# Seven block products instead of eight in two feed-forward expansions, with the inner features kept in DRAM

## Chip, cores and metric

The kernel runs on one core of a Trainium2 chip. The metric is the device time of one execution in microseconds, and the median over runs counts. Everything is float32 in and out, for 1024 tokens of 1024 features.

## What is computed

The program is a chain of three residual blocks. Only the feed-forward ends of the second and third block are touched (D_MODEL = 1024, D_FF = 2816, D_FF_3 = 4096):

```python
# second block
h = h + merged @ w_out[l]
hn = rmsnorm_2(h, norm_ffn[l])
g, up = jnp.split(hn @ w_ffn_in[l], 2, axis=-1)
h = h + (jax.nn.silu(g) * up) @ w_ffn_out[l]
return rmsnorm_2(h, norm_final)

# third block
m = rmsnorm_3(h, norm_mlp_g[l]) @ w_mlp_up[l].astype(h.dtype)
h = h + jnp.square(jax.nn.relu(m)) @ w_mlp_down[l].astype(h.dtype)
out = rmsnorm_3(h, norm_final_g)
```

The product with `w_ffn_in` or `w_mlp_up` is called the expansion here, the one with `w_ffn_out` or `w_mlp_down` the contraction.

## The kernel before

Activations lie feature-major: a tile has 128 features on the partitions and tokens along the row, in two halves `h` of 512 tokens, and eight such tiles `k` make the 1024 features. Every float32 operand of TensorE is split in two parts, a rounded copy (ScalarE, L76 for weights, L151 for activations) and the remainder (VectorE, L77 and L152). `mm3` (L142 to L144) then makes three matmuls of 512 columns per pair of tiles: high by high, high by low, low by high. So a product of one 128-feature output tile with 512 tokens takes 24 matmuls when the inner length is 1024, and 12 when it is 512.

`Weights` streams the weights in the order in which they are used: `load_to` issues a 512 KB load on SyncE's queue into one of two `wraw` buffers, `split_to` makes the two parts in one of four `wsplit` buffers, `get` hands out the next unit and splits one ahead. `gemm_fm` computes expansion units (24 matmuls into a PSUM tile `mm`, of which there are two, then the eviction `evict`); the first `lag` units go over half 0 of the tokens before half 1, since half 1 of the normalised input comes later. `gemm_out` computes the contraction, eight output tiles by two halves, each 3 x nk matmuls, and adds into the residual tiles `u` (L1117, L1480). `seam` is the `gemm_out` that ends a residual part: it takes half 0 completely before half 1, squares and sums each new `u` tile (ScalarE, with the running sum `acc` on GpSimd, L183), and starts `norm_gen` for each half. That makes the row of factors on TensorE (`tp`), copies it to SBUF (`rbc`), multiplies each `u` tile by it (`nt`, VectorE, L301) and splits the result into `xs[k, h]`.

In the second block each hidden tile needs a gate unit and an up unit (L383, L384, L1163), and the contraction follows in groups of 2, 4, 4, 4, 4, 4 hidden tiles (`FF_GROUPS`); one hidden tile of the next group is computed ahead of each group's contraction and the others behind it. In the third block it is eight groups of four, with a squared ReLU (L1497, L1498). Hidden tiles are split as they are made and stay in SBUF until their group is contracted. Residual tiles, `xs` and split hidden tiles take their space from the pools `pg` (28 pages of 4 KB a partition) and `px`.

A scheduler that follows dependencies and priorities writes each engine's instruction order once, ahead of time; evictions have a higher priority (`PRIO_E`). On the chip each engine, and each engine's DMA queue, works strictly in that order.

## Time and profile before

| what | value |
|---|---|
| runs shown, median | 3450.02 us (3443.96, 3450.02, 3455.81) |
| profiled execution | 3442.71 us, with a span of 3441.0 us on the core |
| mean granted TensorE clock | 0.993 |
| TensorE busy (matmul) | 3343.3 us, 16447 records |
| TensorE weight loads | 2730.7 us |
| VectorE / ScalarE / GpSimd busy | 1732.3 / 1054.0 / 249.8 us |
| DMA | 245.06 MB, mean 71 GB/s |

Busy time of TensorE counts overlapping matmuls, so the distance between their starts says more than the busy time of one. The second block's feed-forward part lies at about 1587 to 2297 us of the span, the third block's at about 2700 to 3420 us.

### The profile page before, as it was taken

What the parts mean: (1) busy time and instruction counts of PE and PEld (TensorE: products, weight loads), DVE (VectorE), ACT (ScalarE), POOL (GpSimd) and SP (SyncE); (2) the same over time, 40 slices, a digit from 0 to 9 for tenths busy, and PEclk for the clock granted to TensorE, in tenths of its full rate; (3) what the DMA queues carried; (4) which work ended last, traced back from release to release, by engine and by line L of the source; (5) the groups of instructions that cost most, each with busy time, mean ns of one, the idle gap of its engine ahead of it and who ended that gap; (6) DMA issues with size and microseconds to landing.
All of it is one profiled execution on the core that took longest, in us unless ns stands there. A gap on an engine that the chain in (4) does not pass through costs nothing.

```text
span 3441.0 us, 41019 instructions
## 1 busy us (share of the span) xinstructions
PE 3343.3 (97%) x16447; PEld 2730.7 (79%) x16447; DVE 1732.3 (50%) x3299; ACT 1054.0 (31%) x1853; POOL 249.8 (7%) x239
## 2 busy tenths in 40 slices
PE   6999999999999999999999999999999999999998
PEld 6788877677778888887788888878878788888887
DVE  7465556665655561546332333355569833333334
ACT  5222344433444432213111111144543421121122
POOL 0000000003000000112000000040211200000002
PEclk9999999999999999999999999999999999999999
DMA  5223211322111253421111111121112011111111
GB/s 185 63 99 128 89 51 41 110 68 95 60 40 45 83 166 137 145 80 51 56 49 49 49 49 50 49 95 53 46 50 86 34 53 49 44 48 49 50 49 56
DMA packets 98384, 245.06 MB, mean 71 GB/s; under 512 B 12945, under 2 KB 31505, under 8 KB 98193
## 3 DMA queue, kind: packets, MB, share of 16 engines
q1 hardware_dynamic: 84816, 199.92, 17.0%
q0 software_dynamic: 11360, 39.80, 3.4%
q8 instruction: 129, 2.11, 0.3%
q10 hardware_dynamic: 2016, 2.72, 0.2%
q14 instruction: 63, 0.51, 0.0%
HBM read 196.20 MB, written 46.20 MB: 70 GB/s over the span
## 4 chain that ended last, share of the span: by engine, by line
PE 82%; DVE 8%; issue 7%; ACT 2%; DMA 1%; POOL 0%; POOLq 0%; DVEq 0%; SPq 0%; ACTq 0%
PE mm L142 24%; PE mm L143 24%; PE mm L144 23%; DVE sp L152 1%; PE mm L1614 1%; DVE nt L301 1%; DVE wsplit L77 1%; PE sc L1213 1%; PE tp L1232 1%; PE tp L142 1%; PE tp L143 1%; PE tp L191 1%; PE tp L144 1%; PE sc L934 1%; DVE wsplit L1596 0%
## 5 line engine op out<-in xcount | busy, mean ns | idle before, releaser
L142 PE MATMUL mm<-sp,wsplit 128*128 128x512 f32 x3424 | 1362.0, 398 | 15.7 <-DVE u L1117 4.1
L143 PE MATMUL mm<-sp,wsplit 128*128 128x512 f32 x3424 | 1345.8, 393 | 12.1 <-DVE sp L152 9.6
L144 PE MATMUL mm<-sp,wsplit 128*128 128x512 f32 x3424 | 1343.4, 392 | 0.0
L142 PEld LDWEIGHTS mm<-sp,wsplit 128*128 128x128 f32 x3424 | 645.7, 189 | 157.0 <-issue 6.7
L143 PEld LDWEIGHTS mm<-sp,wsplit 128*128 128x128 f32 x3424 | 646.6, 189 | 144.3 <-DVE sp L152 14.5
L144 PEld LDWEIGHTS mm<-sp,wsplit 128*128 128x128 f32 x3424 | 645.9, 189 | 133.5 <-issue 0.4
L76 ACT CAST wsplit<-wraw 128x1024 fp32r<-128x1024 f32 x264 | 276.8, 1048 | 678.0 <-PE mm L144 632.6
L77 DVE TENSOR_TENSOR wsplit<-wraw,wsplit 128x1024 fp32r<-128x1024 f32 x264 | 330.6, 1253 | 176.2 <-ACT wsplit L76 174.1
L183 POOL TENSOR_TENSOR acc<-acc,sqt 128x512 f32<-128x512 f32 (+1 forms) x105 | 141.1, 1356 | 1523.1 <-ACT sqt L182 1436.5
L143 PE MATMUL mm<-hid,wsplit 128*128 128x512 f32 (+1 forms) x544 | 207.1, 381 | 0.0
L142 PE MATMUL mm<-hid,wsplit 128*128 128x512 f32 (+1 forms) x544 | 206.8, 380 | 0.0
L144 PE MATMUL mm<-hid,wsplit 128*128 128x512 f32 (+1 forms) x544 | 206.3, 379 | 0.0
L1480 DVE TENSOR_TENSOR u<-u,mm 128x512 f32<-128x512 f32 x144 | 98.8, 686 | 184.9 <-PE mm L144 184.6
L1117 DVE SCALAR_TENSOR_TENSOR u<-mm,u 128x512 f32<-128x512 f32 x128 | 88.0, 690 | 170.0 <-PE mm L144 170.0
L1498 DVE TENSOR_TENSOR hd<-hd 128x512 f32<-128x512 f32 x64 | 44.3, 693 | 189.4 <-ACT hd L1497 189.4
L142 PEld LDWEIGHTS mm<-hid,wsplit 128*128 128x128 f32 x544 | 102.2, 188 | 21.2
L143 PEld LDWEIGHTS mm<-hid,wsplit 128*128 128x128 f32 x544 | 102.5, 188 | 20.6
L144 PEld LDWEIGHTS mm<-hid,wsplit 128*128 128x128 f32 x544 | 102.2, 188 | 20.3
L384 DVE SCALAR_TENSOR_TENSOR silu<-silu,mm 128x512 f32<-128x512 f32 x44 | 30.3, 688 | 163.5 <-ACT silu L383 163.5
L1497 ACT ACTIVATE hd<-mm 128x512 f32<-128x512 f32 x64 | 38.3, 598 | 219.6 <-PE mm L144 219.6
L1163 DVE TENSOR_TENSOR silu<-silu,mm 128x512 f32<-128x512 f32 x44 | 30.3, 688 | 127.3 <-PE mm L144 127.3
L383 ACT ACTIVATE silu<-mm 128x512 f32<-128x512 f32 x44 | 26.3, 598 | 183.2 <-PE mm L144 183.2
(515 smaller groups left out, 3732.4 us busy)
## 6 DMA issues: line engine op xcount, KB each, us to landing
wraw<-W SPq DMA_DIRECT2D x264, 512.0 KB, 3.2
x_d<-u SPq DMA_DIRECT2D x32, 256.0 KB, 2.0
t_d<-gl SPq DMA_DIRECT2D x32, 256.0 KB, 2.0
u<-x_d POOLq DMA_DIRECT2D x16, 512.0 KB, 6.0
gl<-t_d POOLq DMA_DIRECT2D x32, 256.0 KB, 3.1
x<-xT SPq DMA_DIRECT2D x16, 256.0 KB, 5.4
u<-xT POOLq DMA_DIRECT2D x8, 512.0 KB, 5.6
bias<-bias POOLq DMA_DIRECT2D x4, 640.0 KB, 4.3
```

The lines of the kernel that those rows point to most:

```text
L76: K.nc.scalar.copy(s[:, 0, :], r)
L77: K.nc.vector.tensor_sub(s[:, 1, :], r, s[:, 0, :].bitcast(F32))
L142: t.matmul(ps, wh, xh, start=first, stop=False)
L143: t.matmul(ps, wh, xl, start=False, stop=False)
L144: t.matmul(ps, wl, xh, start=False, stop=last)
L152: nc.vector.tensor_sub(lo, src, hi.bitcast(F32))
L183: eng.tensor_add(acc, acc, t[:, :acc.shape[-1]])
L191: self.nc.tensor.matmul(ps[:, off + t:off + t + 1], acc[:, t * 128:(t + 1) * 128], self.ones[:, 0:1], start=True, stop=True)
L1117: nc.vector.scalar_tensor_tensor(uu(m, h), ps, 0.5, uu(m, h), op0=OP.mult, op1=OP.add)
L1480: nc.vector.tensor_add(uu(m, h), uu(m, h), ps)
L1497: nc.scalar.activation(t, ps, AF.Relu)
L1498: nc.vector.tensor_mul(t, t, t)
```

## The change

The expansion's weights are seen as blocks of two rows (two output tiles) by two columns (inner features 0 to 511 and 512 to 1023), and the tokens as blocks of two rows (the same feature halves) by two columns (token halves). Each such step of four output blocks needed eight block products of 12 matmuls; in Strassen's scheme in Winograd's form it takes seven, P1 to P7, with sums of blocks as operands. The sums of weights are made on GpSimd for each step (`ssum`, four instructions), those of tokens once per feed-forward part, on VectorE and GpSimd, in place in the `u` tiles (`block_tokens`, T1 to T4). The four outputs C11, C12, C21, C22 share products, so P1, P6, P7 and P4 accumulate in one PSUM tile that is read out in between, and P5 and P3 in half of another; VectorE adds the parts.

The first four units of each part are still computed plainly, with `lag=4`; then come 20 steps in the second block (one hidden tile each, gate and up) and 14 in the third (two hidden tiles each). No contraction stands between them: finished hidden halves go to DRAM (`store`, SyncE's queue), as do the `u` tiles during the seam, since their space is taken for the sums. When all steps are done, `down_loads` brings `u` and the hidden tiles back on GpSimd's queue, splits the latter, and the contractions follow one after the other, each group's loads issued up to one group ahead. The weights' order in DRAM follows. Weight loads for the steps use a third kind of buffer besides `wr` (`paged`).

```diff
+    def take(self, n):
+        j = self.given
+        self.load_to(j + 2 * n)
+        self.given = self.split = j + n
+        return [self.raw.pop(j + i) for i in range(n)]
...
+    def block_tokens(self, u, xs, gens, B, pages):
+        nc = self.nc
+        for k in range(4):
+            B["B11", k], B["B21", k], B["B22", k] = xs[k, 0], xs[k + 4, 0], xs[k + 4, 1]
...
+        for k in range(4):
+            nc.vector.tensor_sub(u(k, 0), u(k, 1), u(k, 0))
+            nc.gpsimd.tensor_sub(u(k, 1), u(k + 4, 1), u(k, 1))
+            part("T1", k, u(k, 0))
...
+        for k in range(4):
+            nc.vector.tensor_sub(u(k + 4, 1), u(k + 4, 1), u(k, 0))
+            nc.gpsimd.tensor_sub(u(k + 4, 0), u(k + 4, 0), u(k + 4, 1))
+            part("T2", k, u(k + 4, 1))
...
+        for n, o, h in (("T3", 0, 1), ("T4", 4, 0)):
...
+    def block_gemm(self, n, B, page, out):
+        nc = self.nc
+        seq = [("P1", 0), ("P5", 0)]
+        for i in range(n):
+            if i + 1 < n:
+                seq += [("P2", i), ("P6", i), ("P3", i), ("P1", i + 1), ("P7", i), ("P5", i + 1), ("P4", i)]
+            else:
+                seq += [("P6", i), ("P3", i), ("P2", i), ("P7", i), ("P4", i)]
+        moving = dict(P1="B11", P2="B21", P3="B22", P4="T4", P5="T1", P6="T2", P7="T3")
...
+            if p == "P5":
+                nc.gpsimd.tensor_add(s, a21, a22)
+                nc.gpsimd.tensor_sub(s3, a11, a21)
+            elif p == "P6":
+                nc.gpsimd.tensor_sub(s, s, a11)
+            elif p == "P3":
+                nc.gpsimd.tensor_sub(s, a12, s)
...
+            self.split(w, o, 512, dict(P1=a11, P2=a12, P4=a22, P7=s3).get(p, s))
...
+            for q in range(len(ready), min(j + 6, len(seq))):
+                ready[q] = operand(q)
...
+            for k in range(4):
...
+                for y, (c, e) in enumerate(((0, 0), (0, 1), (1, 0))):
+                    nc.tensor.matmul(d, wk[:, c, :], xk[:, e, :], start=new and k == y == 0, stop=k == 3 and y == 2,
+                                     skip_group_check=not new)
+            with self.tc.high_priority(offset=PRIO_E):
+                if p == "P1":
+                    nc.scalar.copy(x[:, 0, :], a)
+                elif p == "P5":
+                    nc.scalar.copy(x[:, 1, :], f)
+                elif p == "P2":
+                    nc.vector.tensor_add(x[:, 0, :], x[:, 0, :], b)
...
+                elif p == "P7":
+                    nc.vector.tensor_add(x[:, 1, :], x[:, 1, :], a)
...
+    def down_loads(self, u, u_d, pages, hid, hid_d, groups):
+        nc, m = self.nc, 0
+        for g, n in enumerate(groups):
+            while g > self.down + 1:
+                yield
+            if g < 2:
+                for k in range(4 * g, 4 * g + 4):
+                    u[k] = pages[0](name="ur")
+                    nc.gpsimd.dma_start(u[k], u_d[k])
...
+            for k in range(n):
+                raw.append(pages[1](name="hraw"))
+                nc.gpsimd.dma_start(raw[k], hid_d[m + k])
...
+        self.block_up(uu, xs, gens, B, dict.fromkeys(("T1", "T2", "T3", "T4"), self.split_page), ev_up)
+        for _ in self.block_gemm(20, B, page, out):
+            self.tick()
...
+        dl = self.spawn(self.down_loads(u2, u2_d, (self.xpage, self.page), hid, hid_d, FF_GROUPS))
...
-                up(m0 + n, 1)
                 for _ in self.gemm_out(src3, n, ev_add):
                     self.tick()
-                if FF_GROUPS[gi + 1] > 1:
-                    up(m0 + n + 1, FF_GROUPS[gi + 1] - 1)
...
+        for _ in self.gemm_fm(4, lambda k, h: xs[k, h], ev, lag=4, wait=xs, ahead=False):
+            self.tick()
```

Three places in the instruction order matter. Lines of `mm3`, `split` and `norm_gen` have moved down in the changed file (L142 to L149, L152 to L159, L301 to L436); L358 is the matmul of `block_gemm`.

TensorE, in the middle of the second block's expansion. Before, the end of one unit and the start of the next (`sp_13341`, `sp_13346`: tiles of `xs`):

```order
L142 MATMUL mm_14187<-sp_13619,wsplit_14091 128x512
L143 MATMUL mm_14187<-sp_13619,wsplit_14091 128x512
L144 MATMUL mm_14187<-sp_13619,wsplit_14091 128x512
L142 MATMUL mm_14219<-sp_13341,wsplit_14154 128x512 [waits DVE_49]
L143 MATMUL mm_14219<-sp_13341,wsplit_14154 128x512
L144 MATMUL mm_14219<-sp_13341,wsplit_14154 128x512
```

Now, P5 of one step (`sc_14240`, tokens T1) and P4 of the step before it (`mm_14068`, tokens T4):

```order
L358 MATMUL sc_14240<-sp_13646,wsplit_14123 128x512 x3
L358 MATMUL sc_14240<-sp_13651,wsplit_14123 128x512 x3
L358 MATMUL sc_14240<-sp_13669,wsplit_14123 128x512 x3
L358 MATMUL sc_14240<-sp_13674,wsplit_14123 128x512 x3
L358 MATMUL mm_14068<-sp_13779,wsplit_14160 128x512 [waits DVE_49]
L358 MATMUL mm_14068<-sp_13779,wsplit_14160 128x512 x2
L358 MATMUL mm_14068<-sp_13782,wsplit_14160 128x512 x3
L358 MATMUL mm_14068<-sp_13798,wsplit_14160 128x512 x3
L358 MATMUL mm_14068<-sp_13801,wsplit_14160 128x512 x3
```

A unit of 24 matmuls with one wait has become products of 12; the wait of P4 is for VectorE's read of `mm_14068` after P7, which stands right before this P5.

VectorE, behind the second block's normalisation of half 1. Before, the last normalised tiles are split, and ordinary evictions and weight splits follow:

```order
L301 SCALAR_TENSOR_TENSOR nt_13612<-u2_12359,vec_87,rbc_13539 128x512
L301 SCALAR_TENSOR_TENSOR nt_13617<-u2_12378,vec_87,rbc_13539 128x512 [waits DVE_49]
L152 TENSOR_TENSOR sp_13614<-nt_13612,sp_13614 128x512 [waits Activation_49]
L152 TENSOR_TENSOR sp_13619<-nt_13617,sp_13619 128x512 [waits Activation_49]
L384 SCALAR_TENSOR_TENSOR silu_13482<-silu_13482,mm_13599 128x512 [waits Activation_49]
L77 TENSOR_TENSOR wsplit_13697<-wraw_13411,wsplit_13697 128x1024 [waits DMAHW5_49,PE_49,Activation_49]
```

Now, further down (`wsplit_13823` holds the weights of P1 and P5 of the first step, `wsplit_13830` those of P2 and P6, `sp_13722` belongs to T2, `sp_13739` to `sp_13761` are T3):

```order
L159 TENSOR_TENSOR wsplit_13823<-wraw_13421,wsplit_13823 128x512 [waits DMAHW7_49,PE_49]
L1307 TENSOR_TENSOR silu_13689<-silu_13689,mm_13702 128x512 [waits PE_49]
L159 TENSOR_TENSOR sp_13722<-u2_12378,sp_13722 128x512 [waits Activation_49]
L159 TENSOR_TENSOR sp_13739<-u2_12233,sp_13739 128x512 [waits Activation_49]
L159 TENSOR_TENSOR sp_13742<-u2_12252,sp_13742 128x512 [waits Activation_49]
L159 TENSOR_TENSOR sp_13758<-u2_12275,sp_13758 128x512 [waits Activation_49]
L159 TENSOR_TENSOR sp_13761<-u2_12294,sp_13761 128x512 [waits Activation_49]
L159 TENSOR_TENSOR wsplit_13823<-ssum_13822,wsplit_13823 128x512
L159 TENSOR_TENSOR wsplit_13830<-wraw_13421,wsplit_13830 128x512 [waits Activation_49]
```

The operand of P5, TensorE's second product, has come to stand behind all the sums and splits of T1 to T3.

GpSimd, at the end of the second block's expansion. Before, its queue holds nothing between the running sums of the two seams but one small load:

```order
L183 TENSOR_TENSOR acc_13091<-acc_13091,sqt_13368 128x512 [waits Activation_49,Pool_49]
L183 TENSOR_TENSOR acc_13091<-acc_13091,sqt_13395 128x512 [waits Activation_49]
L183 TENSOR_TENSOR acc_13091<-acc_13091,sqt_13427 128x512 [waits Activation_49,Pool_49]
L183 TENSOR_TENSOR acc_13091<-acc_13091,sqt_13454 128x512 [waits Activation_49]
L1329 DMA mtm_16631<-metat 16x512 [waits DMASW7_49,DVE_49,Pool_49]
```

Now the last step's weight sums are followed by the loads of hidden (`hraw`) and residual (`ur`) tiles:

```order
L330 TENSOR_TENSOR ssum_16194<-wraw2_16061 128x512 [waits DMAHW7_49,DMAHW3_49,DMAHW1_49]
L331 TENSOR_TENSOR ssum_16194<-wraw_16059,wraw2_16061 128x512 [waits DMAHW0_49]
L333 TENSOR_TENSOR ssum_16194<-ssum_16194,wraw_16059 128x512 [waits DVE_49]
L335 TENSOR_TENSOR ssum_16194<-wraw_16059,ssum_16194 128x512 [waits DVE_49]
L394 DMA hraw_16437<-hid2_d_13092 128x1024 [waits DMASW5_49,PE_49]
L394 DMA hraw_16439<-hid2_d_13092 128x1024 [waits DMASW6_49,PE_49]
L390 DMA ur_16429<-u2_d_13091 128x1024 [waits DMAHW6_49,DMAHW5_49,DMASW7_49]
L390 DMA ur_16431<-u2_d_13091 128x1024 [waits DMASW0_49]
```

The first two hidden loads wait for pages that TensorE frees when it has read the tokens of the last P1, eight products before the end of the expansion.

## Rows read from the trace of the kernel before

**Rows 1.** The page: span, and busy time, share and count of each engine

```profile
span 3441.0 us, 41019 instructions
PE 3343.3 (97%) x16447; PEld 2730.7 (79%) x16447; DVE 1732.3 (50%) x3299; ACT 1054.0 (31%) x1853; POOL 249.8 (7%) x239
```

**Rows 2.** Windows: start:end us, length, PE PEld DVE ACT POOL busy, PEclk, DMA, GB/s

```profile
1750.00:2250.00 500.00, 500.00 (x2208) 414.15 (x2207) 162.01 (x202) 82.13 (x107) 0.00 (x0) 1.00 0.14 49
2750.00:3380.00 630.00, 630.00 (x2754) 517.03 (x2753) 225.74 (x287) 124.77 (x174) 0.00 (x0) 1.00 0.14 49
```

**Rows 3.** Timeline of TensorE in the seam before the second feed-forward: start us, us

```profile
1539.79 0.39 PE L143 MATMUL mm<-sp,wsplit 128*128 128x512 f32 x1
...
1561.55 0.39 PE L143 MATMUL mm<-sp,wsplit 128*128 128x512 f32 x1
```

**Rows 4.** Groups of instructions, shapes apart: busy us, mean ns | idle before, releaser

```profile
L152 DVE TENSOR_TENSOR sp<-silu,sp 128x512 fp32r<-128x512 f32 x44 | 30.3, 688 | 15.2 <-ACT sp L151 15.2
L151 ACT CAST sp<-silu 128x512 fp32r<-128x512 f32 x44 | 27.2, 618 | 103.5 <-DVE silu L1163 103.5
L383 ACT ACTIVATE silu<-mm 128x512 f32<-128x512 f32 x44 | 26.3, 598 | 183.2 <-PE mm L144 183.2
L183 POOL TENSOR_TENSOR acc<-acc,sqt 128x512 f32<-128x512 f32 x91 | 130.9, 1452 | 1507.7 <-ACT sqt L182 1421.0 <-ACT acc L179 86.1
```

**Rows 5.** Timelines of VectorE and GpSimd in the later seam, and behind it

```profile
2303.78 1.77 DVE L152 TENSOR_TENSOR sp<-nt,sp 128x512 fp32r<-128x512 f32 x1
2307.17 0.68 DVE L152 TENSOR_TENSOR sp<-nt,sp 128x512 fp32r<-128x512 f32 x1
2311.87 0.68 DVE L1117 SCALAR_TENSOR_TENSOR u<-mm,u 128x512 f32<-128x512 f32 x1
2334.34 1.89 DVE L152 TENSOR_TENSOR sp<-nt,sp 128x512 fp32r<-128x512 f32 x3
...
2303.56 3.14 POOL L183 TENSOR_TENSOR acc<-acc,sqt 128x512 f32<-128x512 f32 x2 [0.25 <-ACT sqt L182]
2309.25 3.83 POOL L183 TENSOR_TENSOR acc<-acc,sqt 128x512 f32<-128x512 f32 x2 [2.56 <-ACT sqt L182]
```

**Rows 6.** Windows of 20 us around the starts of both feed-forward parts

```profile
1580.00:1600.00 20.00, 18.34 (x84) 14.32 (x83) 16.03 (x32) 6.39 (x11) 3.36 (x2) 1.00 0.14 51
1600.00:1620.00 20.00, 19.63 (x87) 15.86 (x86) 15.39 (x33) 9.37 (x16) 1.56 (x3) 1.00 0.18 60
1620.00:1640.00 20.00, 20.00 (x90) 16.58 (x89) 4.99 (x8) 3.79 (x6) 0.00 (x0) 1.00 0.16 53
2700.00:2720.00 20.00, 18.55 (x78) 14.35 (x76) 18.24 (x30) 8.97 (x14) 6.77 (x5) 0.95 0.14 52
2720.00:2740.00 20.00, 18.28 (x83) 14.25 (x83) 16.73 (x34) 9.14 (x16) 1.81 (x1) 1.00 0.09 27
```

**Rows 7.** DMA issues: queue, count, KB each, median us to landing; then GpSimd's issue time

```profile
wraw<-W SPq DMA_DIRECT2D x264, 512.0 KB, 3.2
x_d<-u SPq DMA_DIRECT2D x32, 256.0 KB, 2.0
u<-x_d POOLq DMA_DIRECT2D x16, 512.0 KB, 6.0
...
L320 POOL DMA_DIRECT2D u<-x_d x16 | 8.6, 539 | 43.2 <-PE tp L1302 35.6 <-ACT lma L1718 6.6 <-DVE sp L152 0.8
```

More of the change, by code (lines that the diff above doesn't have):

```diff
@@ L216, in gemm_fm @@
                 ws.append(self.W.get())
-            elif i == lag + 1 and lag > 1:
+            elif i == lag + 1 and lag > 1 and ahead:
                 self.W.split_to(self.W.given + 1)
@@ L607, in ev @@
                     h, uu, v(g), xs, acc[:, s], acc2[:, s] if fg is not None else None,
-                    v(fg) if fg is not None else None, spill and spill[8], LEAD[g])))
+                    v(fg) if fg is not None else None, spill[8] if fg is not None else None, LEAD[g], stay)))
         for _ in self.gemm_out(src, nk, ev, by_half=True, gate=gate):
@@ L1168, in up, with store @@
[L1168 to L1172 removed]
+        u2_d, hid_d = D("u2_d", 8), D("hid2_d", 22)
+        xs, gens = self.seam(u2, lambda k, h: mg[k, h], 4, ev_add, None, "norm_ffn_2", u2_d, stay=True)
+        def store(m, h, t):
+            nc.sync.dma_start(hid_d[m][:, h * 512:h * 512 + 512], t)
+        B = {}
+        px = ExitStack()
+        extra = px.enter_context(tc.tile_pool(name="px2x", side="right", bufs=3))
@@ new lines, in page, with ev_up @@
+        def page(shape=(128, 1024), name="pg"):
+            pool = extra if name == "wraw2" or (name == "ssum" and not B.get("s")) else self.px
+            B["s"] = name == "ssum" or B.get("s")
+            return pool.tile(list(shape), F32, name=name, tag="px")
+        for i in range(20):
+            self.W.paged[self.W.given + 5 + 2 * i] = lambda: page(name="wraw2")
+        at = {}
+        def ev_up(i, h, ps):
+            m, what = divmod(i, 2)
+            if what == 0:
+                at[m, h] = self.half_tmp("silu")
+                self.silu2(at[m, h], ps)
+            else:
+                t = at[m, h]
+                nc.vector.tensor_mul(t, t, ps)
+                store(m, h, t)
@@ L1189, in block2, with block_up, blocks @@
         return u2, r
+    def block_up(self, u, xs, gens, B, pages, ev):
+        def blocks():
+            while any(g in self.sides for g in gens):
+                yield
+            yield from self.block_tokens(u, xs, gens, B, pages)
+        tg = self.spawn(blocks())
+        for _ in self.gemm_fm(4, lambda k, h: xs[k, h], ev, lag=4, wait=xs, ahead=False):
+            self.tick()
+        self.finish(tg, *gens)
     def att_tile(self, hp, j, qd, kd, vd, bias, att_d):
@@ L1498, in ev, with page @@
                 nc.vector.tensor_mul(t, t, t)
-                hid[base + i, h] = (self.page if (base + i) % 4 == 0 else self.xpage)((128, 2, 512), F32R, "hid")
-                self.split(hid[base + i, h], 0, 512, t)
-            return ev
-        def up(m0, n, lag=1):
-            for _ in self.gemm_fm(n, src2, ev_up(m0), lag=lag, wait=xs):
-                self.tick()
-        up(0, 4, LAG)
-        self.finish(*gens)
+                store(4 + 2 * i + 1, 0, t)
+            else:
+                relu2(4 + 2 * i + (block == "C22"), block != "C11", t, t)
+        B, hid = {}, {}
+        xsp = lambda: self.xpage((128, 2, 512), F32R, "sp")
+        self.block_up(uu, xs, gens, B, dict(T1=self.split_page, T2=xsp, T3=xsp, T4=self.split_page), ev_up)
+        first = [self.xpage, self.xpage]
+        def page(shape=(128, 1024), name="pg"):
+            return (first.pop() if first else self.page)(shape, F32, name)
+        for _ in self.block_gemm(14, B, page, out):
+            self.tick()
+        self.down = 0
+        self.spawn(self.down_loads(u3, u3_d, (self.page, self.xpage), hid, hid_d, (4,) * 8))
         for gi in range(8):
```

154 lines of the change are left out of this document (105 added, 49 removed).

## The prediction
> **What bounds the kernel now.** I read the page first: TensorE is busy in 97% of a span of 3441.0 us, no other engine in more than 50% [rows 1]. Since matmuls overlap, that share alone proves little, so next the stretches. In both feed-forward parts TensorE starts a matmul every 0.23 us without a gap (2208 records in 500 us, 2754 in 630 us), at a granted clock of 1.00, while VectorE works a third of the time, ScalarE a sixth to a fifth and GpSimd not at all [rows 2]. The timeline gives the step exactly: from the first row shown to the last are 96 matmuls in 21.76 us, so 0.2267 us for one of 512 columns [rows 3]. The stretch of the third block alternates products of 24 matmuls and of 12, that of the second likewise, and the mean is the same 0.226 to 0.229 us: short products cost nothing extra, as long as their waits are over. So here time is the number of matmuls, and whatever else is added is free until it makes TensorE wait.
>
> **What is removed.** Each step saves one block product of 12 matmuls. 20 + 14 steps make 34 x 12 = 408 (the orders count 16,021 matmuls before, 15,613 now; the contraction keeps its own). 408 x 0.2267 = **92.5 us**, all on the path.
>
> **What a step adds.** A step now lasts 84 x 0.2267 = 19.0 us on TensorE. Beside it VectorE makes 7 remainder splits, 3 additions from PSUM and 4 finishing operations: 14 x 0.69 = 9.7 us. ScalarE makes 7 casts, 3 copies and up to 2 activations: 7 x 0.62 + 5 x 0.60 = 7.3 us. GpSimd makes 4 sums, 4 x 1.45 = 5.8 us [rows 4]. None reaches 19.0. But GpSimd and VectorE disturb each other. While GpSimd adds, a split of 0.68 us takes 1.77 us, and one behind GpSimd's work 0.68 again; an addition that reads PSUM beside GpSimd's 3.83 us keeps its 0.68 [rows 5]. So each GpSimd sum costs VectorE about 1.09 us, and a step 9.7 + 4 x 1.09 = 14.1 us: still hidden. Operands are prepared six products (16.3 us) ahead, so a late GpSimd sum is not seen either.
>
> One wait in a step is short. P4 must wait until VectorE has added P7's result out of the same PSUM tile, and only P5 (12 x 0.2267 = 2.72 us) lies between. The addition takes 0.69; one undisturbed split ahead of it makes 1.4, one that GpSimd has hit makes 1.77 + 0.69 = 2.5 us. So a step loses 0 as a rule, and some tenths where two disturbed operations stand ahead. Nearest the rows is nothing; I charge 2 us for all 34 steps and keep 34 us (1 us each) as the upper end. If this cover were gone, each step would lose up to the 2.5 us. Behind P4 in TensorE's queue stand all other products, so what it loses is not made up.
>
> **What the starts add.** The sums of the token blocks must be ready at P5, the second block product. In the second block I count 42 VectorE instructions in its order from the first normalised tile of half 1 to the operand of P5. Three in a row take 1.89 us, so one adds 0.60 [rows 5]: 25 us. In that time GpSimd has 8 token sums and 3 weight sums, at 1.09 each 12 us more if each hits a split: 25 to 37 us. TensorE has to work meanwhile on two units of half 0, four of half 1 and P1, 156 x 0.2267 = 35.4 us. So between 0 and 2 us are lost by the count, and a few more if TensorE's own clock starts late; I take 2, up to 5. In the third block it is 47 instructions and up to 13 sums, 28 to 42 us, against 153 matmuls, 34.7 us: 0 to 8 us. I take 5, up to 12 since evictions of earlier work hang on here. When P5 waits, everything on TensorE waits. ScalarE has 8 + 16 casts and evictions there, under 20 us, and hides. The larger `lag` gives something back: the part's starts lose now (90 - 87) and (90 - 83) matmuls of a full window, 2.3 us together [rows 6], and a unit of 24 more matmuls as cover should save most of it: minus 2, between 0 and minus 2.3.
>
> **What the way through DRAM adds.** A hidden half goes out in 2.0 us, a tile comes back in 6.0 us over GpSimd's queue, which takes 0.54 us for each issue [rows 7]. In a contraction group of four, 192 matmuls or 43.5 us long, four tiles (4 x 6.0 even one after the other) and 8 splits pass beside it, issued one group ahead: hidden. SyncE's queue carries two weight loads of 512 KB (3.2 us) and two to four stores (2.0 us) in 19.0 us; the stores wait for VectorE, and weight loads behind them are needed only a step later. The spill of `u` in the seams, 16 x 2.0 us on SyncE's queue, also stands ahead of weight loads, in some 43 us of TensorE work. Exposed are the two handovers. The first loads may go when the last P1 is done, 8 products or 21.8 us before the end; issue, 6.0 us, and two splits make 9 us. The eighth residual tile comes last, behind four hidden loads, about 0.54 x 5 + 6.0 = 9 us or, if the transfers run one by one, 30 us after the pages are free, for an addition that is due 19 us into the first group: 0 to 11 us in the second block. The third block has twice that time. Nearest to a measured load is 9 us, so I take 2 us for each handover, up to 11 and 5.
>
> **Sum:** -92.5 + 2 (steps) + 2 + 5 (starts) - 2 (lag) + 4 (handovers) = **-81.5 us**. The profiled execution took 3442.7 us, span 3441.0, so its like would take 3361. It is 7.3 us below the median of the runs shown; on the median's base the forecast is 3450.0 - 81.5 = **3368 us**. Runs of this kernel differ by 0.3% or so, 10 us, which is what a measurement can tell from no change.
>
> **A rule against the change.** The page "SBUF — State Buffer" of the Trainium skill, section "Who interferes with whom", says that VectorE instructions with two SBUF inputs and GpSimd instructions that read SBUF hold a shared port in turn, for a whole instruction, and the one that comes second waits for all of it. The case's trace agrees in kind: the two-input split is held, the one with a PSUM input is not [rows 5]. By the rule at its worst VectorE would lose each GpSimd sum entirely, and how often that falls into the short wait before P4 is the first rival.
>
> **Rivals.**
> *The steps stall on VectorE (0.12).* Were each of GpSimd's four sums (1.45 us) lost to VectorE in full, a step would be 9.7 + 5.8 = 15.5 us of 19.0: not the bound, but the queue is long enough that P7's addition often stands behind two disturbed operations, 2 x 1.77 + 0.69 = 4.2 against 2.72 us, so 1 to 1.5 us lost in each step: 34 to 51 us, time 3400 to 3418. For it: GpSimd's sums come in pairs. Against: in the order the addition usually has one split ahead of it, and evictions take precedence.
> *All is covered (0.12).* The starts, steps and handovers lose nothing: -92.5 and the 2.3 of the lag, time 3355. For it: the seams shown lose only a few matmuls even with VectorE at 80% [rows 6]; against, the count of VectorE's work above.
> *The contraction starves (0.05, the slower side).* In place of hidden tiles that lie in SBUF, each group now needs loads whose pages must come free first, in GpSimd's strict order. If a group's loads were only released by the end of the group before it, each of the 5 + 7 later groups would wait 6.0 + 4 x 0.54 + 0.62 + 0.69 = 9.5 us, 114 us in all: 3368 + 114 = 3482 us. It decides from 81.5 / 12 = 6.8 us of wait in a group. For it: two raw and split copies compete for 28 pages. Against: loads run a group, 43.5 us, ahead.
> *The saving isn't one (0.03).* If TensorE took longer for each matmul of the steps, by 0.2267 x 408 / (34 x 84) = 0.03 us, nothing would remain: 3450. Against: same shape, same columns, the same three passes [rows 3], and weight parts that are loaded the same way.
>
> **How the numbers follow.** The forecast has 0.68. Its own range, from all starts and handovers free to all at their upper ends (12 + 5 + 16 in place of 11), is -92.5 to -59: 3357 to 3391. The range for 8 in 10 takes in the covered case on the profiled execution's base (3350, and 4 for the runs' spread) and the lower part of the stalled steps: **3346 to 3402**. Faster by over 0.3%: 0.68 + 0.12 + 0.12 = 0.92. Within 0.3%: 0.04, slower 0.04, from the last two rivals, of which a little of the starved case falls between.
>
> **What would show it.** After: 408 fewer matmuls, and in the middle of both expansions 220 matmul records in 50 us at a clock of 1.00; VectorE there at 65 to 80%, GpSimd near 30%. TensorE's waits for VectorE: some at the first P5 and P2 of each part, few microseconds in total at P4. A window in a contraction with clearly fewer records, or a wait on a DMA of hidden tiles, speaks for starvation; 34 equal gaps of about 1 us before P4 speak for the stalled steps. Wrong is the forecast if the steps' windows hold under 210 records, or if more than 20 us are lost outside of them.

## The result, and the profile after

Before, the median is 3448.57 us (3443.96 to 3455.81); with the change 3388.69 us (3385.71 to 3390.70). The ratio is 0.9824, 95% interval 0.9805 to 0.9843: 60 us less, where 81.5 less was forecast; 3388.7 lies in the upper part of the range of 3346 to 3402. The two profiled executions, 3442.7 and 3385.7 us with spans of 3441.0 and 3383.9 us, differ by 57.0 us in time and 57.1 in span, so the accounts below, which are read from these two traces, have to come to 57. The medians and intervals in this document leave out two executions of 6487 us, one of each of two later kernels.

The page after; it answers to [rows 1]: TensorE has exactly the 408 records fewer that the sum starts from (16447 - 16039).

```profile
span 3383.9 us, 41750 instructions
PE 3266.0 (97%) x16039; PEld 2666.3 (79%) x16039; DVE 1937.2 (57%) x3619; ACT 1169.3 (35%) x2115; POOL 510.2 (15%) x461
```

Where did the rest go? Windows of 50 us, after; columns as in [rows 2]. A window that loses nothing holds 222 matmul records, in the expansion of the third block 220 or 221.

```profile
1550.00:1600.00 50.00, 45.84 (x205) 36.75 (x203) 34.71 (x58) 17.30 (x26) 17.02 (x13) 0.97 0.30 105
1600.00:1650.00 50.00, 46.78 (x197) 37.45 (x196) 46.93 (x59) 23.41 (x42) 21.52 (x13) 0.97 0.15 50
1650.00:1700.00 50.00, 50.00 (x223) 41.39 (x222) 26.93 (x37) 18.46 (x34) 15.61 (x11) 1.00 0.24 83
1750.00:1800.00 50.00, 50.00 (x222) 41.39 (x221) 25.19 (x37) 17.09 (x31) 12.68 (x9) 1.00 0.24 80
2000.00:2050.00 50.00, 45.75 (x189) 35.94 (x189) 41.24 (x88) 26.50 (x46) 10.46 (x20) 0.97 0.87 328
2650.00:2700.00 50.00, 43.10 (x178) 34.31 (x178) 37.23 (x62) 18.72 (x29) 18.23 (x13) 0.90 0.30 105
2700.00:2750.00 50.00, 40.29 (x158) 32.03 (x158) 42.09 (x50) 21.54 (x39) 30.55 (x17) 0.91 0.22 76
2750.00:2800.00 50.00, 50.00 (x217) 40.89 (x216) 26.39 (x36) 15.75 (x28) 15.82 (x12) 0.99 0.35 121
2850.00:2900.00 50.00, 50.00 (x220) 41.06 (x219) 24.98 (x36) 16.39 (x29) 15.35 (x12) 1.00 0.35 120
3000.00:3050.00 50.00, 46.35 (x191) 37.66 (x190) 27.45 (x38) 13.56 (x21) 9.59 (x19) 0.93 0.78 307
```

The same stretches before, in the same view (the seams and starts; beyond them its windows hold 222 or 223 in the second block and 218 to 222 in the third):

```profile
1550.00:1600.00 50.00, 46.77 (x213) 37.45 (x212) 36.49 (x63) 19.46 (x30) 14.88 (x10) 1.00 0.12 42
1600.00:1650.00 50.00, 49.63 (x219) 40.72 (x218) 23.42 (x44) 14.40 (x24) 1.56 (x3) 1.00 0.17 56
1650.00:1700.00 50.00, 48.40 (x211) 38.77 (x210) 24.62 (x33) 10.04 (x12) 0.00 (x0) 1.00 0.19 64
2650.00:2700.00 50.00, 44.22 (x204) 34.48 (x204) 40.96 (x65) 23.08 (x30) 13.28 (x9) 0.99 0.10 33
2700.00:2750.00 50.00, 46.83 (x204) 36.77 (x203) 42.72 (x74) 23.71 (x38) 8.57 (x6) 0.98 0.10 35
2750.00:2800.00 50.00, 50.00 (x221) 41.02 (x220) 19.91 (x25) 11.08 (x16) 0.00 (x0) 1.00 0.18 60
```

Four places lose. Start of the second block: 213 + 219 + 211 = 643 records before, 625 after, 18 x 0.2267 = 4.1 us. Start of the third block: 629 and 553, 76 records, 17.2 us. Handover of the second block: 222 - 189 = 33, 7.5 us. Handover of the third: 222 - 191 = 31, 7.0 us. Together 35.8; 92.5 - 35.8 = 56.7 of the 57.1 that the spans show. The steps (1750, 2850) lose nothing beyond what the same stretches lost before, so what the change costs lies in the starts and handovers. That the sum meets the spans so closely is partly chance. Followed matmul by matmul, the execution shown after is already 3.4 us behind where the second block's seam begins to sum its squares (`tp<-ones,acc` at 1562.7 us before, 1566.1 after), in work that the change leaves alone; and the third block wins back some 4 us that no window above has, since its contractions now hold 222 records and before, mixed with the expansion, 218 to 222.

What TensorE waits for there: engine, tile and line, then the releaser, microseconds in total, times, the longest. The first two rows are of 1580 to 1660, the next four of 2670 to 2780, the next three of 1995 to 2060, the last of 2985 to 3045.

```profile
PE mm L149 <- ACT sp L158: 3.6, 2, 3.1
PE mm L149 <- DVE silu L1307: 3.1, 1, 3.1
...
PE mm L358 <- ACT scp L362: 5.0, 1, 5.0
PE mm L149 <- ACT sp L158: 3.8, 2, 3.1
PE mm L149 <- ACT hd L1672: 3.6, 1, 3.6
PE mm L358 <- ACT hd L1672: 1.1, 1, 1.1
...
PE mm L149 <- DVE ur L1252: 2.4, 2, 1.8
PE sc L358 <- DVE c L372: 1.3, 1, 1.3
PE mm L358 <- DVE scp L375: 0.5, 1, 0.5
...
PE mm L149 <- ACT hd L1679: 3.7, 1, 3.7
```

In the third block's three windows the waits sum to 16.6 us (the 13.5 shown, and nearly all of the rest ahead of 2670), but 113 records or 25.6 us are missing there, 17.2 more than before. Windows of 2 us around one of the waits show the difference; the eighth column of figures, before the DMA share, is the granted clock:

```profile
2682.00:2684.00 2.00, 0.00 (x0) 0.00 (x0) 2.00 (x3) 0.62 (x1) 0.77 (x1) 0.76 0.69 210
2684.00:2686.00 2.00, 1.98 (x5) 1.59 (x6) 2.00 (x3) 0.62 (x1) 0.00 (x0) 0.50 0.16 64
2686.00:2688.00 2.00, 2.00 (x6) 1.55 (x5) 0.32 (x1) 0.00 (x0) 0.00 (x0) 0.50 0.75 264
2688.00:2690.00 2.00, 2.00 (x6) 1.58 (x5) 0.19 (x1) 0.60 (x1) 0.00 (x0) 0.53 0.02 6
2690.00:2692.00 2.00, 2.00 (x14) 1.78 (x14) 0.55 (x2) 0.00 (x0) 0.00 (x0) 1.00 0.32 121
```

TensorE stands for 3.1 us, then works for some 6 us at 0.50, the lower of its two levels (1.2 GHz), with 5 or 6 matmuls in 2 us and not 9. Counted by their starts, 14 matmuls lie in the three windows from 2684 to 2690 and not 26 (the rows add up to 17 because a matmul across an edge counts on both sides): 12 x 0.2267 = 2.7 us more, for one wait of 3.1. A low clock follows the waits of 3.6 and 5.0 us here too, that of 3.1 in the second block and that of 3.7 in the third handover. It follows some shorter ones as well: that of 1.8 us in the second handover, and one of 1.9 us in the third block's seam, there in the trace of before already.

### The profile page after: what moved, and what is told of

Same layout as the page of the kernel before. It is cut to its first block, busy times and chain, and to the rows that moved or that the text cites. A ratio compares the mean times of both kernels' runs of the same rounds, so it can differ in the third digit from the quotient of the medians.

```text
span 3383.9 us, 41750 instructions
## 1 busy us (share of the span) xinstructions
PE 3266.0 (97%) x16039; PEld 2666.3 (79%) x16039; DVE 1937.2 (57%) x3619; ACT 1169.3 (35%) x2115; POOL 510.2 (15%) x461
## 5 line engine op out<-in xcount | busy, mean ns | idle before, releaser
L149 PE MATMUL mm<-sp,wsplit 128*128 128x512 f32 (+1 forms) x2880 | 1151.0, 400 | 30.0 <-ACT sp L158 9.7
L150 PE MATMUL mm<-sp,wsplit 128*128 128x512 f32 (+1 forms) x2880 | 1132.4, 393 | 9.5 <-DVE sp L159 7.1
L151 PE MATMUL mm<-sp,wsplit 128*128 128x512 f32 (+1 forms) x2880 | 1129.7, 392 | 0.0
L149 PEld LDWEIGHTS mm<-sp,wsplit 128*128 128x128 f32 x2880 | 547.1, 190 | 149.2 <-ACT sp L158 14.1
L358 PE MATMUL mm<-sp,wsplit 128*128 128x512 f32 x1632 | 390.5, 391 | 6.6 <-ACT scp L362 5.0
L76 ACT CAST wsplit<-wraw 128x1024 fp32r<-128x1024 f32 x196 | 205.7, 1049 | 494.3 <-PE mm L151 468.3
L358 PEld LDWEIGHTS mm<-sp,wsplit 128*128 128x128 f32 x1632 | 306.5, 188 | 73.5 <-ACT scp L362 5.4
L77 DVE TENSOR_TENSOR wsplit<-wraw,wsplit 128x1024 fp32r<-128x1024 f32 x196 | 244.8, 1250 | 152.7 <-ACT wsplit L76 145.1
L358 PE MATMUL sc<-sp,wsplit 128*128 128x512 f32 x1224 | 296.6, 391 | 1.3 <-DVE c L372 1.3
L358 PEld LDWEIGHTS sc<-sp,wsplit 128*128 128x128 f32 x1224 | 231.1, 189 | 51.0 <-DVE c L372 1.7
L190 POOL TENSOR_TENSOR acc<-acc,sqt 128x512 f32<-128x512 f32 (+1 forms) x105 | 140.1, 1346 | 474.9 <-ACT sqt L189 388.3
L1646 DVE TENSOR_TENSOR ur<-ur,mm 128x512 f32<-128x512 f32 x112 | 76.8, 686 | 152.1 <-PE mm L151 152.1
L159 DVE TENSOR_TENSOR wsplit<-ssum,wsplit 128x512 fp32r<-128x512 f32 x136 | 101.8, 750 | 89.1 <-ACT wsplit L158 88.9
L1252 DVE SCALAR_TENSOR_TENSOR ur<-mm,ur 128x512 f32<-128x512 f32 x96 | 66.2, 689 | 106.5 <-PE mm L151 106.3
L158 ACT CAST wsplit<-ssum 128x512 fp32r<-128x512 f32 x136 | 82.9, 621 | 109.8 <-POOL ssum L335 36.0
L159 DVE TENSOR_TENSOR sp<-hraw,sp 128x512 fp32r<-128x512 f32 x108 | 71.3, 686 | 11.6 <-ACT sp L158 11.6
```

The costliest lines, as they stand in the source:

```text
L76: K.nc.scalar.copy(s[:, 0, :], r)
L77: K.nc.vector.tensor_sub(s[:, 1, :], r, s[:, 0, :].bitcast(F32))
L149: t.matmul(ps, wh, xh, start=first, stop=False)
L150: t.matmul(ps, wh, xl, start=False, stop=False)
L151: t.matmul(ps, wl, xh, start=False, stop=last)
L158: nc.scalar.copy(hi, src)
```

## The experiments

Times are medians; the ratio to the kernel before, measured side by side, stands with its interval. The half-widths are 0.0013 to 0.0019, 5 to 7 us, and the median of the kernel before itself lay between 3448.57 and 3451.64 us, so for smaller differences the windows decide, each of one execution. Where an edit packed a choice into one line, its cut is written out here over several.

**1. Who makes the token sums.** In the third block's start GpSimd took 2.95 us for each of its first four token sums, and VectorE was busy without a break.

```diff
-            nc.gpsimd.tensor_sub(u(k, 1), u(k + 4, 1), u(k, 1))
+            nc.vector.tensor_sub(u(k, 1), u(k + 4, 1), u(k, 1))
...
-            nc.gpsimd.tensor_sub(u(k + 4, 0), u(k + 4, 0), u(k + 4, 1))
+            nc.vector.tensor_sub(u(k + 4, 0), u(k + 4, 0), u(k + 4, 1))
```

> Edit: the eight token sums that GpSimd makes at the start of each part are made on VectorE instead; everything else as in the changed kernel (3388.7 us). Theory A (the starts are late because GpSimd's sums hold VectorE, at about 1.1 us for each, and because sums and evictions stand in one strict order): VectorE loses 8 x 0.6 = 4.8 us of its own work in each start but is hit eight times less (8.7 us) and waits for no partner; the waits for silu L1307 (3.1 us) and hd L1672 (3.6 us) fall below 2 us each, the time by 4 to 12 us, most in the third block, where the GpSimd sums took 2.95 us each. Theory B (VectorE simply has too much work in the starts, whoever disturbs it): the added 4.8 us per start show as 0 to 5 us more wait in each, 0 to 10 us slower. No change within 2 us would mean that the sums' engine does not matter and the order of the evictions does.

Measured: 3378.31 us, ratio 0.9795 (0.9781 to 0.9810), 10.4 us faster: theory A. The waits of TensorE at both starts (second block, then third):

```profile
PE mm L149 <- ACT sp L158: 3.6, 2, 3.1
PE sc L358 <- ACT scp L364: 2.3, 1, 2.3
PE mm L358 <- DVE silu L1307: 0.3, 1, 0.3
...
PE mm L149 <- ACT sp L158: 3.8, 2, 3.1
PE sc L358 <- ACT scp L364: 1.8, 1, 1.8
```

Those for hd and for the reading of P1 (scp L362) are gone, that for silu is 0.3 us, and small ones of 1.4 and 0.4 us for weight splits have come up in the third block; the two seam waits of 3.1 us stand, as they must, since they lie before the token sums. The third block's window from 2700 holds 197 records in place of 158.

**2. More PSUM targets at the starts.** The last two plain units of half 1 write to the halves of one `sc` tile.

```diff
-            ps = self.mm()
+            if not ahead and h == 1 and u in (2, 3):
+                fb = self.sc() if u == 2 else fb
+                ps = fb[:, u % 2 * 512:u % 2 * 512 + 512]
+            else:
+                ps = self.mm()
```

> Edit: of the four plain units of half 1 the last two go to the two halves of an sc PSUM tile, so that TensorE has four PSUM targets there and not two. Theory A (TensorE waits because evictions stand behind the token sums in VectorE's and ScalarE's order, not because of operands): the waits of 3.1 us for silu L1307 and of 3.6 us for hd L1672 vanish and are not made up elsewhere, 5 to 8 us faster. Theory B (VectorE is full from the normalisation to the operand of P5, so the end of its queue is what counts): the waits move to P1, P5 or P2 for splits or copies, same sum, change within 2 us.

Measured: 3391.27 us, ratio 0.9832 (0.9817 to 0.9846), 2.6 us slower and within the intervals: theory B. The waits at the two starts moved:

```profile
PE sc L149 <- DVE silu L519: 5.1, 1, 5.1
...
PE mm L358 <- DVE wsplit L159: 2.5, 1, 2.5
...
PE sc L149 <- ACT hd L1672: 6.6, 1, 6.6
PE mm L358 <- DVE wsplit L159: 3.8, 1, 3.8
```

A PSUM tile more lets TensorE run one unit further, up to the next thing that is owed to it. In the third block that is an eviction of ScalarE, and the casts ahead of it wait for VectorE's token sums (u L300). This fits VectorE's queue as a whole as the bound, not the place of one eviction in it; the late eviction was the symptom.

**3. More cover.** Six plain units, one step fewer in each part (19 in the second block, 13 in the third).

```diff
-        for _ in self.gemm_fm(4, lambda k, h: xs[k, h], ev, lag=4, wait=xs, ahead=False):
+        for _ in self.gemm_fm(6, lambda k, h: xs[k, h], ev, lag=4, wait=xs, ahead=False):
...
-        for _ in self.block_gemm(20, B, page, out):
+        for _ in self.block_gemm(19, B, page, out):
```

> Edit: six plain units before the steps instead of four, 19 and 13 steps instead of 20 and 14. Price: 2 x 12 matmuls x 0.2267 = 5.4 us. Each part gets 4 x 24 matmuls (21.8 us) of TensorE work between the normalisation and P1, which needs no token sum. Theory A (the starts lack cover): the part of the starts' excess behind the seam wait, about 4 us in the second block and 13 us in the third, goes, so 6 to 12 us faster net. Theory B (evictions behind the sums hold the two PSUM targets, whatever follows): four more evictions are queued there, nothing is gained, 4 to 8 us slower.

Measured: 3382.42 us, ratio 0.9808 (0.9794 to 0.9823), 6.3 us faster, with intervals that overlap. By the windows theory A holds in the third block (197 records from 2700 to 2750 in place of 158), B in the second (199 from 1600 to 1650, 197 without the edit). With the token sums on VectorE as well:

> Edit: the token sums on VectorE (which alone gave 3378.3 us) and six plain units before the steps with 19 and 13 steps (which alone gave 3382.4 us). Theory A (both edits mend the same loss, the late operands and evictions of the starts, so they don't add up): after the sums are on VectorE the waits behind the seam are 2.6 us in the second block and 5.2 us in the third; two units more can save those at most and cost 5.4 us: 3376 to 3380 us. Theory B (they mend different losses and add up): 3388.7 - 10.4 - 6.3 = 3372 us.

Measured: 3377.10 us, ratio 0.9787 (0.9773 to 0.9802). The time is that of theory A, but the reason is not. At the starts the edits do add up: the windows from 1600 and 2700 hold 224 and 219 records, with the token sums alone on VectorE 214 and 197, and with the windows from 1550 and 2650 some 10 us come back there for a price of 5.4 (six plain units alone: 36 records, 8 us). What was won is lost at the second block's handover, where TensorE now waits 7.9 us for ur L1252 and not 2.8:

```profile
2000.00:2050.00 50.00, 42.11 (x173) 32.60 (x172) 38.01 (x83) 23.25 (x41) 9.95 (x19) 0.97 0.82 312
```

With the token sums alone this window holds 195 records, 22 more, 5.0 us. Why the handover got worse no run shows.

**4. The handovers.** First the second group's loads were held back:

```diff
+            old = raw if g == 1 else []
...
-                raw.append(pages[1](name="hraw"))
+                raw.append(old[k] if k < len(old) else pages[1](name="hraw"))
```

> Edit: the second contraction group's hidden loads reuse the tiles of the first group's loads, so they start only when those are split, in both handovers; two of four tiles in the second block, all four in the third. Theory A (the handovers lose because all loads start at once and fill the DMA engines at 400 GB/s, so that the first group's tiles land after 9 to 13 us and not 6, and casts that wait for them block evictions): the first group's tiles land in 6 to 8 us, the waits for hd L1679 (3.65 us) and ur L1252 (1.8 us) shrink, 3 to 7 us faster in all. Theory B (the strict order of ScalarE and VectorE there is the cause, and the traffic is not): no change within 2 us, or up to 6 us slower where the second group's tiles then come late.

Measured: 3387.90 us, ratio 0.9821 (0.9804 to 0.9837): no change. Between 2985 and 3045 the wait for hd L1679 (3.7 us) went and one of 3.2 us for ur L1646 came. Hidden tiles still took 11.3 us to land (12.8 without the edit): the loads of the third and fourth group, whose pages are free, took the place of the second's. The next two, with the token sums on VectorE, left the loads alone and gave more cover or more PSUM:

```diff
-FF_GROUPS = (2, 4, 4, 4, 4, 4)
+FF_GROUPS = (4, 4, 2, 4, 4, 4)
```

> Edit: token sums on VectorE, and contraction groups of 4, 4, 2, 4, 4, 4 hidden tiles in the second block in place of 2, 4, 4, 4, 4, 4. Theory A (the first group is too short to cover the reload of the residual tiles and of the second group): with 192 matmuls and not 96 in the first group the waits for ur L1252 in the second block (2.8 us) fall below 1 us, 2 to 4 us faster than 3378.3. Theory B (what stands ahead in VectorE's order is the cause there): the waits stay, within 2 us; a group of two later on costs nothing or little, since the earlier groups give it time.

Measured: 3380.06 us, ratio 0.9802 (0.9786 to 0.9818). The waits for ur vanished and one of 5.3 us for scp L1319, the last P4's reading, took their place: within 2 us, as B has it, though the window from 2000 holds 181 records, with the token sums alone 195.

```diff
-            ps = self.mm()
+            if wide and i < 4:
+                fb = self.sc() if i % 2 == 0 else fb
+                ps = fb[:, i % 2 * 512:i % 2 * 512 + 512]
+            else:
+                ps = self.mm()
```

> Edit: token sums on VectorE, and the first four units of each contraction go to the four halves of the sc PSUM tiles, which the steps no longer need, so that TensorE need not wait until the last P4 is read out. Theory A (in the third block's handover only the late reading of one PSUM tile, hd L1679, holds TensorE): its wait of 6.1 us goes, 4 to 6 us faster than 3378.3. Theory B (the hidden tiles' splits that wait for DMA stand ahead of all evictions, so the wait moves to the next product whose PSUM tile or operand is late, as it did with more PSUM targets at the starts): within 2 us.

Measured: 3376.83 us, ratio 0.9789 (0.9772 to 0.9805). In the third block the wait for hd (6.1 us) became one for ur L1646 of 5.4 us: theory B. What all of these share stands in ScalarE's order at the third handover, here of the changed kernel itself (start, microseconds, in brackets idle time before and its releaser):

```profile
3014.49 1.14 ACT L158 CAST sp<-hraw 128x512 fp32r<-128x512 f32 x2 [4.56 <-DMA hraw<-hid_d]
3016.56 1.14 ACT L158 CAST sp<-hraw 128x512 fp32r<-128x512 f32 x2 [0.94 <-DMA hraw<-hid_d]
3017.61 0.59 ACT L1679 ACTIVATE hd<-mm 128x512 f32<-128x512 f32 x1
```

The tiles of the first group, which are needed, had landed by 2999.4. These are casts of the second group, not needed for 40 us; they wait for their loads, and the eviction that TensorE waits for stands behind them. So the fourth edit took them out of that place by a dependency: from the second group on, hidden tiles are loaded into the T4 tiles, which the last P4 still reads.

```diff
-                raw.append(pages[1](name="hraw"))
-                nc.gpsimd.dma_start(raw[k], hid_d[m + k])
+                raw.append(B["T4", k].bitcast(F32) if g else pages[1]((128, 2, 512), F32, "hraw"))
+                for h in (0, 1):
+                    nc.gpsimd.dma_start(raw[k][:, h, :], hid_d[m + k][:, h * 512:h * 512 + 512])
```

> Edit: token sums on VectorE, and the hidden tiles of the second and all later groups are loaded into the four T4 tiles, which the last P4 of the steps reads; so they are not loaded, and their casts can't be put into ScalarE's order, before the steps are done (and each group's loads follow the splits of the group before; loads are issued in halves of 256 KB). Theory A (the handovers lose because casts and splits of the second group, waiting for loads on full DMA engines, stand ahead of the last evictions): the wait for hd L1679 (6.1 us) falls below 1 us, hidden tiles of the first group land in 5 to 8 us, 4 to 8 us faster than 3378.3. Theory B (the loss is the way through DRAM itself: the first tiles and the residual tiles come too late anyway): the waits move to the first group's splits or to ur, within 2 us. Against both: the second group could come late, up to 10 us slower.

Measured: 3378.28 us, ratio 0.9796 (0.9781 to 0.9810): no change in sum, but the two handovers, second block and third, went opposite ways:

```profile
2000.00:2050.00 50.00, 43.32 (x173) 33.80 (x172) 37.55 (x91) 22.16 (x36) 13.28 (x25) 0.93 0.77 272
3000.00:3050.00 50.00, 48.55 (x213) 39.27 (x212) 25.38 (x35) 10.70 (x15) 8.56 (x16) 1.00 0.56 200
```

With the token sums alone on VectorE these windows hold 195 and 187 records. In the third block 26 x 0.2267 = 5.9 us came back and the wait for hd is gone: theory A holds there. The edit also thinned the traffic (200 GB/s in that window, 273 without it), so the strict order and the full DMA engines are not parted by it. In the second block 22 records, 5.0 us, were lost; TensorE waited 4.9 us there for one ur.

**5. Work inside the wait.** Twelve matmuls into an unused PSUM tile, to see whether the low clock can be bought off.

```diff
+                if i == 0 and k == 6:
+                    for z in [self.sc()[:, :512]] * 12:
+                        self.nc.tensor.matmul(z, ws[u][:, 0, :128], src(0, h)[:, 0, :512], start=True, stop=True)
```

> Edit: token sums on VectorE, and ahead of the product in each start for which TensorE waits 3.1 us in the seam (feature tile 6 of the first plain unit of half 0), 12 matmuls of 512 columns that compute nothing needed, into an sc PSUM tile: 2.7 us of work inside the wait. Theory A (a wait costs more than its length: after each of 3 us and more the granted clock is 0.50 for some 4 us, during which 2 us hold 5 to 6 matmuls and not 9): with TensorE kept at work the clock stays at 1.00 behind both seams, the first products still start when their operand is there, 3 to 6 us faster than 3378.3. Theory B (the wait alone counts, and the lower clock has another cause): no change within 2 us. Against both: if the operand were ready before the filler ends, up to 1 us slower.

Measured: 3383.29 us (3378.39 to 3391.15), ratio 0.9802 (0.9786 to 0.9819). Inconclusive, and no gain. In the second block the clock stayed at 1.00 up to 1598 us, past the filled wait; but further splits were late too (waits of 1.2 and 0.7 us), and after them it fell to 0.63 and 0.52 all the same. In the third block a wait of 3.3 us for a split stayed. What a low clock costs is read from the windows above; that it can be bought off is not shown.

**6. The seam's running sums on VectorE.** The seam waits come before the token sums, yet in the trace of before the seam of the second block has no wait over 1.1 us. There, as at the starts, VectorE is without slack and GpSimd adds beside it, in both kernels. From the first normalised tile of half 0 to the last of its splits VectorE takes 18.2 us before (from 1569.05) and 21.0 after (from 1572.36); the eight normalisations make 7.9 us of it before and 9.6 after, the eight splits 6.1 and 7.2. Why more of them are held after the change no run shows.

```diff
-            self.square_sum(acc[:, s], uu(m, h), m == 0, eng=nc.gpsimd)
+            self.square_sum(acc[:, s], uu(m, h), m == 0, eng=nc.vector if stay else nc.gpsimd)
```

> Edit: token sums on VectorE, and in the two seams ahead of the feed-forward parts the running sums of squares are added on VectorE too, not on GpSimd. Theory A (as with the token sums, a VectorE that has no slack is better off doing GpSimd's additions itself, since each of them holds it by 1.1 us and its own cost is 0.6 us): the seam waits of 3.1 us for sp L158 fall below 1.5 us, 3 to 6 us faster than 3378.3 with the clock that comes back. Theory B (in the seam the additions mostly fall beside evictions that read PSUM and are not held, so VectorE only gets 16 additions more in each seam, 14 x 0.6 = 8 us): the waits grow, 2 to 10 us slower.

Measured: 3370.43 us, ratio 0.9769 (0.9755 to 0.9784), 7.9 us faster than with the token sums alone: theory A, beyond its range. VectorE's groups from 1565 to 1600, first with the token sums alone on VectorE (busy us and mean ns behind the bar):

```profile
L436 DVE SCALAR_TENSOR_TENSOR u<-u,vec,rbc 128x512 f32<-128x512 f32 x8 | 9.6, 1232 | 0.1
L159 DVE TENSOR_TENSOR sp<-u,sp 128x512 fp32r<-128x512 f32 x8 | 7.2, 951 | 0.0
```

then with the running sums there too:

```profile
L436 DVE SCALAR_TENSOR_TENSOR u<-u,vec,rbc 128x512 f32<-128x512 f32 x8 | 5.8, 746 | 0.0
L190 DVE TENSOR_TENSOR acc<-acc,sqt 128x512 f32<-128x512 f32 x8 | 5.5, 688 | 0.8 <-ACT sqt L189 0.8
L159 DVE TENSOR_TENSOR sp<-u,sp 128x512 fp32r<-128x512 f32 x8 | 5.2, 686 | 0.0
```

Eight additions cost 5.5 us, and the sixteen others got 5.8 us shorter: an even trade in busy time. But the splits were also spread differently in the order, and the last two of half 0 ended at 1595.1 us and not at 1598.1. In the third block TensorE's wait of 1.9 us for GpSimd's running sum itself (acc L190) went too, so a part of the gain there may be a shorter chain and not a VectorE that is held less. Both seam waits vanished, and with them the low clock behind them (windows of 1550 and 2650, with both edits):

```profile
1550.00:1600.00 50.00, 49.89 (x230) 40.95 (x229) 37.83 (x73) 18.66 (x28) 1.28 (x1) 1.00 0.34 117
2650.00:2700.00 50.00, 48.37 (x220) 38.40 (x219) 47.59 (x88) 23.11 (x37) 3.02 (x2) 1.00 0.32 111
```

The kernel before has such running sums, and that wait of 1.9 us, too; no run puts them on VectorE there, so how much of the 7.9 us needs the change is open.

**7. What held, together.** Token sums and running sums on VectorE, and the T4 loads in the third block alone:

> Edit: token sums and the two seams' running sums on VectorE (3370.4 us), and, in the third block alone, the second and later groups' hidden tiles loaded into the T4 tiles, so that they can't be loaded or cast before the steps end. Theory A (each handover's loss is set by the order in which casts and splits that wait for DMA stand ahead of evictions; in the second block the T4 tiles came too late behind a first group of only two, in the third they have twice the time): the third block's handover again keeps 25 matmuls more in 100 us, as it did in that earlier run there, 5 to 6 us faster: 3364 to 3366 us. Theory B (what is won at the handover is lost again when the later groups wait for their loads): 3369 to 3373 us.

Measured: 3361.49 us, ratio 0.9739 (0.9725 to 0.9752), 8.9 us faster: theory A by the time, beyond its range. No trace of this kernel shows its handover; that of the next one does. With six plain units in the third block:

> Edit: the same, and in the third block six plain units and 13 steps. Theory A (the third block's start still lacks cover, 35 matmuls or 8 us in 50 us): up to 6 us less wait for 2.7 us more matmuls, 2 to 4 us faster than the kernel before it in this call. Theory B (with both seams and token sums on VectorE the start is as good as covered, the rest are single waits of 1 to 3 us that move): 0 to 3 us slower than it.

Measured: 3359.07 us, ratio 0.9730 (0.9717 to 0.9744), 92.6 us less than before, whose median beside it was 3451.64. The third handover of this one loses next to nothing:

```profile
3000.00:3050.00 50.00, 50.00 (x221) 40.88 (x220) 27.27 (x39) 13.73 (x20) 8.58 (x16) 1.00 0.47 165
```

The last 2.4 us are within the intervals of the two and not shown apart from them.

## Why the prediction was right, and where it was too hopeful

**What is removed: right.** 408 records fewer, at the rate of [rows 3]: 92.5 us. By its own sign of being wrong, more than 20 us lost outside the steps, the forecast failed all the same: 35.8 us were lost there. The starts and handovers add up to 33 us at the upper ends that it gave them, so that 3388.7 still lies below the 3391 of its own range is partly luck.

**The steps: right, and better than charged.** 2 us were charged; the windows at 1750 and 2850 hold 222 and 220 records at a clock of 1.00, as asked for. VectorE works 50% of the time, not 65 to 80%. Each GpSimd sum was priced at one held split [rows 5]; in fact GpSimd works 12.7 to 15.4 us in those windows, and VectorE's means there are 686 to 742 ns for splits; of the finishing operations only the one that makes `c` stands out with 1188. With VectorE half idle most sums seem to fall beside nothing that they could hold. The page "SBUF — State Buffer" of the Trainium skill, section "Who interferes with whom", has the two sides exclude each other for a whole instruction. That fits the third block's start, where both queues are full: GpSimd's first token sums take 2.95 us there and VectorE's operations beside them 1.75 to 1.78. In the steps the queues are not full. So the rival "the steps stall" fell: from 1660 to 1995 and from 2755 to 2985 the trace has no wait of TensorE, and its only wait at P4 is one of 0.5 us, in the second handover.

**The starts: the step that failed.** The text had 2 + 5 - 2 = 5 us for them; the traces show 4.1 + 17.2 = 21.3. Three things were mis-sized:

- *What stands in the seam.* The gain of 2 us from a larger `lag` did not show. Of TensorE's waits for splits in the second block's seam one became 3.1 us long, in the third block likewise. Experiment 6 removed both by taking GpSimd out.
- *Whose work is late.* The count of VectorE's work up to P5's operand was fair: it took 33.6 us in the second block (1600.8 to 1634.4; 25 to 37 forecast) and 39.9 in the third (2696.1 to 2736.0; 28 to 42). Not fair was the end to which it was held: TensorE has no wait for P5's operand in either start. Evictions stand in the same queue, or on ScalarE behind casts that wait for it, and TensorE stops at the first thing owed, not the last (silu L1307, hd L1672, then the reading of P1, scp L362). Nor was GpSimd's own side counted: it is held as well, 2.95 us for a sum that takes 1.29 us in the steps at its shortest. Experiment 1 gave 10.4 us back, 2 speaks against the order of one eviction as the cause, and 3 shows that cover helps, most in the third block.
- *What a wait costs.* A wait was charged at its length. After each of the waits of 3.1 to 5.0 us at the starts the clock is 0.50 for some 3 to 7 us; at half the rate that is an estimated 1.7 to 3.1 us on top, 2.7 by the count above.

**The way through DRAM: right in kind, 4 us charged for the handovers, 14.5 measured.** The contractions don't starve: past the handovers they hold 221 to 223 records. In the handover the loads were costed by a landing time of 6.0 us; with the DMA engines full (about 410 GB/s from 3005 to 3035) hidden tiles land after a median of 12.8, the last two of the second group after 12.1 and 13.6. Of my upper ends, 11 and 5, the first held the 7.5 us, the second not the 7.0. But in the third block the larger part of the price is one that I had not named, ScalarE's strict order: casts of a group that isn't needed yet stand ahead of the evictions that are. The T4 edit, which takes them out of there and thins the traffic, gave 5.9 us back. In the second block the cause is open: VectorE's order there has 33 small operations of the third block's setup ahead of `c`, for which TensorE waits 1.3 us; no edit here removed the loss, and three made it larger (six plain units with the token sums on VectorE, other groups, the T4 loads).

**The sum.** Steps 0 and not 2, starts 21.3 and not 5, handovers 14.5 and not 4: 35.8 and not 11 to be taken off 92.5. The rival "all is covered" is wrong for this kernel. The last experiment, with 92.6 us, comes close to its gain but doesn't bear it out: its 33 steps remove 396 matmuls, 89.8 us, its second handover still lacks 35 records (187 from 2000 to 2050), and what makes up for that are seam waits that the kernel before has too.

## What to carry to other kernels

When a change fills VectorE at a few places, look there for GpSimd working beside it: where VectorE has no slack, doing GpSimd's additions on VectorE was the faster way twice, while in the half-idle steps GpSimd's help was free. Price a long wait of TensorE with the slow stretch behind it: here those of 3.1 to 5.0 us cost some 2 to 3 us more. And look at what waits for loads that may start early, since in a strict order it holds up what doesn't: tying them to the event after which they are wanted gave 5.9 us at one handover, but the same edit lost 5.0 at the other. Last, when two edits together bring no more than one, read where: here both gains stood, and a third place had lost them.

## What the runs showed that was not expected

- One wait of 3.1 us in the third block's seam is followed by some 6 us at a granted clock of 0.50; in the trace of before, four waits of 0.38 to 1.04 us in a row in the second block's seam leave it at 1.00, while one of 1.9 us in the third block's does not.
- Being held works both ways: a GpSimd addition of two 128x512 tiles takes 1.29 us in the steps at its shortest, 1.45 in the seams of before [rows 4], and 2.95 at the third block's start, where VectorE's queue is full.
- A 512 KB load on GpSimd's queue lands after 6.0 us in the kernel before [rows 7], after 12.8 with all the handover's loads in flight at about 410 GB/s.
